# Mixer: the gelus of five returned tiles move a round later, and six weight sums move from the gated unit to the second feed-forward's first pairs

## The chip, the cores and the metric

The kernel runs as one program on one core of a Trainium2 chip. The metric is device time in microseconds. The core has five engines with a queue of instructions each, run in order: TensorE (PE), VectorE (DVE), ScalarE (ACT), GpSimd (POOL) and SyncE (SP). DMAs are issued from the queues of SP, ACT and POOL. The page lists PE's weight loads apart, as PEld.

## The reference

One step of a two-layer streaming encoder in float32 over 1088 positions (1024 of a prompt and 64 of a sample), with D = 1024 channels and a feed-forward of 2816. Layer 0 mixes positions by windowed attention. Layer 1, which the change touches, mixes them by a complex diagonal recurrence (64 groups, 64 states each), then a gelu and a gated linear unit. Each layer ends with a gated feed-forward that has a causal convolution of width 3 on its up-projection.

```python
y = <recurrence over positions> + d_skip * h
z = gelu(y)
ag = z @ w_glu + b_glu
out = ag[..., :D_MODEL] * sigmoid(ag[..., D_MODEL:])
...
up = h @ w_up
c = conv_b + sum(conv_w[j] * shifted(up, j) for j in range(3))
y = (gelu(c[..., :D_FF]) * c[..., D_FF:]) @ w_down
```

Norms (RMS) stand before and after each mixer and each feed-forward.

## The kernel before, in words

**Stages.** In order: attention (layer 0), its feed-forward, the recurrence of layer 1 (in the profile 1190 to 1290 us), the gated unit (1290 to 1493), the second feed-forward's up-projection (from 1493), its down-projection. Every product splits its operands into a high and a low half (hh/hl, zh/zl; weights whl) and runs three matmuls for one (L233 to L235, L1485). Positions go in three blocks of 384, 384 and 320 columns.

**The recurrence.** `ssm` runs batches of two group pairs through a generator, `batch` (L1283 to L1425). The runner `staged` takes every live generator one step per round, the oldest first, so each `yield` puts what follows it behind one more round of all the others. A batch goes through DVE (L1327, L1332, L1333, the scan at L1344, L1347, L1348) with matmuls on PE before (L1293) and after (L1356, L1362, accumulators p3, four buffers). ACT takes p3 out into `ys` (L1370). Every second batch completes a tile of 128 channels, kt = 0 to 7: `ys` is stored to `yd` from ACT's queue (L1377), two yields later it is loaded back in another layout as `yf` by SP (L1383, one yield less for the last tiles), one yield later ACT makes the gelu `z` (L1400 and a small one at L1403), then the high halves `zh` (three copies, L1409); DVE makes the low halves `zl` one yield later (L1424). Tiles 3, 4 and 5 (LATE) leave their `zl` until after the last batch. `ys`, `yf`, `z` of the other tiles, the sums' `sj` and the unit's `sg` all come from one pool, t4, with five buffers, which they take in turn: a new tile waits until the one before it in its buffer has been read by all.

**The gated unit.** 24 tiles (8 columns m by 3 blocks b), 40 to 48 matmuls each (L1485), then a sigmoid `sg` on ACT (L1500) and `y` on DVE (L1501). The last three columns go block by block, so block 0 ends with six tiles to go. At a block's end ACT squares y (sqa, L264), DVE adds the squares (L266, L270) and PE sums them over channels (pr, L276); in PE's order pr stands behind the first matmuls of the next tile. Ahead of each tile and half tile stands one call of `beside` (L1459), which starts one weight sum and finishes one started earlier. A weight sum, `sums(f, e)`, loads two slices of the second feed-forward's up weights on POOL's queue (`sj`, L1446), combines them by four operations of DVE (L1450 to L1453) and stores them to `su` (L1454). The second feed-forward's later pairs use seven products for eight, and read `su` as weights (raw<-su); pairs f = 0 to 4 (PLAIN = 5) are plain. There are 34 sums: f = 5 to 21, two each.

**The second feed-forward.** `gate` (L466) runs once per pair f = 0 to 21. PE makes up-projections into accumulators `mm` (six buffers); DVE takes them out into `u` (L446, L448); the convolution is one operation of ACT and two of DVE (L454 to L456); after the gelu (L469) and the product (L472), POOL stores the result to `gd` (L473, L474). Each convolution is followed by `aside` (L478), which is the place for side work: sums of the down weights, started at given numbers of asides and finished one or two asides later (`sums(j)`, L417, with a table of jobs). In the plain pairs 3 and 4 DVE also forms the normed inputs (L499, L510) and their halves (L492) for the pairs of seven products (L528), which use small pools' tiles t2, t10, t11 among others.

Of the kernel before, what the change touches and what calls it, by code (L numbers as in the profile page):

```python
# [8 lines left out]
F32 = mybir.dt.float32  # L9
# [6 lines left out]
P = 128  # L16
# [6 lines left out]
KF = DFF // P  # L23
# [5 lines left out]
PLAIN = 5  # L29
# [15 lines left out]
class Core:  # L45
# [326 lines left out]
    def ffn(self, i, h, rb, after, side=None, beside=lambda: None, x=None, g=None):  # L372
# [41 lines left out]
        starts.update({2 * (k + KH) + 2: sums_g(k) for k in range(KH)})  # L414
        jobs = {}

        def sums(j):  # L417

            for x in jobs.pop(j, []):
                next(x, None)  # L420
            if j in starts:
                x = starts[j]
                next(x)
                jobs[j + 1 + i] = [x]

        def u_tile(m):
            u = self.t4([P, T + 4], "u")
# [50 lines left out]
        def aside():  # L478

            j = next(turns) + 1  # L480
            if side is not None and j <= SIDE:
                with self.later(LOW):
                    next(side, None)
            sums(j - 1)


        def half(v, j):
# [73 lines left out]
        else:  # L561
            ts_ctx = tc.tile_pool(name="ts", bufs=1)
            ts = ts_ctx.__enter__()
# [673 lines left out]
    def ssm(self, after):  # L1237
# [4 lines left out]
        with tc.tile_pool(name="ss", bufs=1) as sp:  # L1242
# [39 lines left out]
            def batch(qs):  # L1282
# [17 lines left out]
                for c in range(2):  # L1300
                    x = nc.scalar.activation(sc[:, :, c], pm[:, :, OSI:PRM], AF.Copy, scale=(1.0, -1.0)[c])
                    if out[0]:
                        self.order(x, out[0])
                for e, q in enumerate(qs):
                    x = nc.scalar.activation(rd[:, e], mask[:, None, :].to_broadcast([P, 2, 138]), AF.Copy, scale=self.rho[:, q:q + 1])
# [21 lines left out]
                x = nc.vector.tensor_mul(A[:, :, :, 1:], cos[:, :, :, 1:], p1)  # L1327
# [7 lines left out]
                for q in qs:  # L1335
                    if q % 4 == 0 and q < 28:
                        k = q // 4 + 1
                        x = self.ssm_scale(us[k // 2], 8 * (k % 2), 8 * (k % 2) + 8)
# [13 lines left out]
                for i, q in enumerate(qs):  # L1352
                    p3 = [x[:, i] for x in po]
                    for e in range(2):
                        o = OKT + P * e
                        x = nc.tensor.matmul(p3[e], pm[:, i, o:o + P], U(2 * q + e), start=True, stop=False)  # L1356
                    f = self.fill(p1s[-1][:, 0, 2 * NC_:], 1, 512 - 2 * NC_, x) if i == 0 else None
# [17 lines left out]
                if qs[-1] % 4 == 3:  # L1375
                    kt = qs[-1] // 4
                    out.append(nc.scalar.dma_start(yd[kt * P:kt * P + P].rearrange("(g i) t c -> (i t) g c", i=16), ys[0]))  # L1377
                    if kt < 7:
                        yield
                    if kt < 6:  # L1380
                        yield
                    yf = self.t4([P, 8, NC_], "yf")
                    x = nc.sync.dma_start(yf, yd[kt * P:kt * P + P])  # L1383
                    yfs.append(x)
                    self.order(x, got[max(got)])
                    if kt < 7:
                        yield
                    if kt == 6:
                        yield

                        yield
                    if kt == 7:
                        yield
                        yield
                    if kt == LATE[1]:
                        z = self.prep2.tile([P, 2, T], F32, name="z", tag="p2", bufs=1)
                        late[:] = [z[:, x] for x in range(2)]
                    z = late[kt - LATE[1]] if kt in LATE[1:] else self.t4([P, T], "z")
                    yv = yf.rearrange("p t c -> p c t")
                    x = nc.scalar.activation(z[:, 0:SEQ].rearrange("p (c t) -> p c t", t=8), yv[:, 0:128], AF.Gelu_apprx_tanh)  # L1400
                    self.order(x, out[0])
                    self.order(x, out[-1])
                    x = nc.scalar.activation(z[:, SEQ:].rearrange("p (c t) -> p c t", t=8), yv[:, 129:137], AF.Gelu_apprx_tanh)  # L1403
                    self.order(x, out[0])
                    self.order(x, out[-1])
                    for b, (t0, n_) in enumerate(BLK):
                        if kt == 0:
                            zh[b], zl[b] = self.bt(self.blk, b, "zh", F32R), self.bt(self.blk, b, "zl", F32R)
                        nc.scalar.activation(zh[b][:, kt], z[:, t0:t0 + n_], AF.Copy)  # L1409
                    if kt in LATE:  # L1410
                        zs[kt] = z
                        return
                    if kt < 7:
                        yield
                    for b in range(3):
                        x = lower(b, kt, z)
                        if kt < 7:
                            self.order(x, adds[-1])
# [20 lines left out]
        ws = {}  # L1439
        su = self.su = self.dram.tile([KF, 2, P, 2, 512], F32, name="su")  # L1440

        def sums(f, e):

            x = self.t4([P, 2, 2, 256], "sj")
            for j in range(2):
                nc.gpsimd.dma_start(x[:, j], a["w_up"][1, j * KF + f].rearrange("p (c q) -> p c q", c=2)[:, :, 256 * e:256 * e + 256])  # L1446
            yield
            a11, a12, a21, a22 = x[:, 0, 0], x[:, 0, 1], x[:, 1, 0], x[:, 1, 1]
            V = nc.vector
            V.tensor_add(a22, a21, a22)  # L1450
            V.tensor_sub(a21, a11, a21)
            V.tensor_sub(a11, a22, a11)
            V.tensor_sub(a12, a12, a11)  # L1453
            nc.gpsimd.dma_start(su[f, e], x.rearrange("p j c q -> p j (c q)"))  # L1454

        jobs = iter([sums(f, e) for f in range(PLAIN, KF) for e in range(2)])
        loaded = []

        def beside():  # L1459
# [213 lines left out]
```

## Time and profile before

| what | us |
|---|---|
| median of 3 runs (lowest, highest) | 2233.78 (2233.59, 2239.8) |
| the profiled execution | 2242.03 |
| its span on the core | 2240.2 |
| PE, DVE, ACT, POOL busy in it | 2198.9, 1658.0, 1045.6, 410.1 |
| granted clock of PE, mean | 0.993 |

The times in the prediction come from the profiled execution, which took 8.25 us more than the median; 1.8 us of it lie outside the span. In a timeline row stand the start, the busy time, the engine, the line, the operation, what it writes and reads, and how often; in brackets the idle time of the engine just before it and what ended that. In a row of the stretches stand the span, then busy us (and instructions) of PE, PEld, DVE, ACT and POOL, the granted clock, the mean busy share of the 16 DMA engines and GB/s. A group row ends with the summed idle time before its instructions and what ended it. Line numbers are those of the kernel before; in the changed kernel they are 8 to 11 higher.

### The profile page before, as it was taken

Reading aid. Unit: us, or ns where it says so; the run is one execution under the profiler, and the core shown is the slowest. Engines: PE = TensorE matmul, PEld = TensorE weight load, DVE = VectorE, ACT = ScalarE, POOL = GpSimd, SP = SyncE. Lnnn points to the kernel's source line nnn. Section 1 sums busy time; section 2 is a strip of 40 time slices with the busy share of each in tenths; the row PEclk is TensorE's granted clock in tenths of the full one; section 3 lists DMA queues with packets and bytes.
Section 4 is the critical chain, followed back from the end, with each engine's and each line's share of the span. In section 5 each row is a group of like instructions: output and inputs, shape, how many; then the busy total and the mean of one; then the engine's idle time right before and its main releaser. Section 6 shows DMA issues by size and latency. Waiting matters only on the chain.

```text
span 2240.2 us, 36047 instructions
## 1 busy us (share of the span) xinstructions
PE 2198.9 (98%) x13899; PEld 2121.8 (95%) x13899; DVE 1658.0 (74%) x2885; ACT 1045.6 (47%) x1896; POOL 410.1 (18%) x472
## 2 busy tenths in 40 slices
PE   8999999999999999999999899999999999999999
PEld 8987789999999999999986799999999999999998
DVE  8687648989878877767758865588976776676763
ACT  5256747422343342555534741263555455455543
POOL 5322004200132423000200044352010110110000
PEclk9999999999999999999999999999999999999999
DMA  5100015655355565887749888652266686578773
GB/s 197 37 22 29 20 62 158 247 187 202 116 155 173 169 209 186 275 279 230 233 163 344 254 307 291 235 167 75 87 220 233 218 301 222 196 267 312 221 250 102
DMA packets 208123, 428.47 MB, mean 191 GB/s; under 512 B 23312, under 2 KB 114224, under 8 KB 205008
## 3 DMA queue, kind: packets, MB, share of 16 engines
q1 hardware_dynamic: 175648, 326.56, 44.2%
q0 software_dynamic: 23984, 95.12, 11.9%
q10 hardware_dynamic: 8320, 4.49, 0.8%
q8 instruction: 109, 1.79, 0.3%
q14 instruction: 62, 0.51, 0.1%
HBM read 297.75 MB, written 128.37 MB: 190 GB/s over the span
## 4 chain that ended last, share of the span: by engine, by line
PE 29%; DMA 16%; DVE 8%; issue 5%; ACT 3%; POOL 1%; SPq 0%; ACTq 0%; DVEq 0%; POOLq 0%
PE mm L233 9%; PE mm L235 9%; PE mm L234 9%; DMA raw<-in_w_down 4%; DMA sj<-in_w_up 3%; DMA jw<-in_w_down 2%; DMA yf<-yd 1%; DVE whl L222 1%; PE pb L1485 1%; PE pa L1485 1%; ACT whl L221 1%; DMA gr<-gd 1%; DMA pm<-prm 1%; DMA raw<-sd 1%; DVE t L456 1%
## 5 line engine op out<-in xcount | busy, mean ns | idle before, releaser
L233 PE MATMUL mm<-hl,whl 128*128 128x384 f32 (+1 forms) x1960 | 643.0, 329 | 4.0 <-DVE hl L316 2.8
L235 PE MATMUL mm<-hh,whl 128*128 128x384 f32 (+1 forms) x1960 | 640.8, 328 | 2.3 <-DVE whl L222 2.3
L234 PE MATMUL mm<-hh,whl 128*128 128x384 f32 (+1 forms) x1960 | 642.9, 328 | 0.0
L233 PEld LDWEIGHTS mm<-hl,whl 128*128 128x128 f32 x1960 | 368.5, 188 | 6.2 <-DVE hl L316 4.6
L235 PEld LDWEIGHTS mm<-hh,whl 128*128 128x128 f32 x1960 | 368.3, 188 | 3.0 <-DVE whl L222 2.9
L234 PEld LDWEIGHTS mm<-hh,whl 128*128 128x128 f32 x1960 | 368.8, 188 | 0.1
L222 DVE TENSOR_TENSOR whl<-raw,whl 128x1024 fp32r<-128x1024 f32 x202 | 253.7, 1259 | 149.9 <-ACT whl L221 146.5
L221 ACT ACTIVATE whl<-raw 128x1024 fp32r<-128x1024 f32 x202 | 213.1, 1058 | 253.2 <-PE mm L235 131.3
L233 PE MATMUL mm<-gt,whl 128*128 128x384 f32 (+1 forms) x968 | 318.4, 329 | 4.5 <-ACT whl L221 2.9
L235 PE MATMUL mm<-gt,whl 128*128 128x384 f32 (+1 forms) x968 | 316.8, 328 | 0.4 <-DVE whl L222 0.4
L234 PE MATMUL mm<-gt,whl 128*128 128x384 f32 (+1 forms) x968 | 317.0, 328 | 0.0
L233 PEld LDWEIGHTS mm<-gt,whl 128*128 128x128 f32 x968 | 182.7, 189 | 5.7 <-ACT whl L221 3.2
L235 PEld LDWEIGHTS mm<-gt,whl 128*128 128x128 f32 x968 | 182.3, 188 | 1.3 <-DVE whl L222 1.3
L234 PEld LDWEIGHTS mm<-gt,whl 128*128 128x128 f32 x968 | 182.7, 189 | 0.0
L196 DVE TENSOR_TENSOR whl<-raw,whl 128x1024 fp32r<-128x1024 f32 x84 | 96.3, 1153 | 76.5 <-ACT whl L195 75.9
L195 ACT ACTIVATE whl<-raw 128x1024 fp32r<-128x1024 f32 x84 | 82.7, 987 | 105.7 <-DMA raw<-sd 40.7
L455 DVE SCALAR_TENSOR_TENSOR t<-u,ppt,t 128x1090 f32<-128x1090 f32 x88 | 126.7, 1441 | 6.3 <-ACT t L454 4.5
L454 ACT ACTIVATE t<-u,ppt 128x1090 f32<-128x1090 f32 x88 | 114.3, 1298 | 23.9 <-DVE u L551 12.7
L456 DVE SCALAR_TENSOR_TENSOR t<-u,ppt,t 128x1090 f32<-128x1090 f32 x88 | 121.7, 1383 | 0.4
L469 ACT ACTIVATE t<-t 128x1090 f32<-128x1090 f32 x44 | 49.0, 1115 | 114.9 <-DVE t L456 114.8
L446 DVE TENSOR_TENSOR u<-rb,mm 128x384 f32<-128x384 f32 (+1 forms) x164 | 80.2, 501 | 30.4 <-PE mm L235 25.6
L595 DVE TENSOR_TENSOR gt<-gr,gt 128x768 fp32r<-128x768 f32 (+2 forms) x106 | 90.2, 879 | 9.9 <-ACT gt L594 9.4
(392 smaller groups left out, 4072.2 us busy)
## 6 DMA issues: line engine op xcount, KB each, us to landing
raw<-in_w_up SPq DMA_DIRECT2D x88, 512.0 KB, 4.3
raw<-in_w_down SPq DMA_DIRECT2D x74, 512.0 KB, 4.4
raw<-sd SPq DMA_DIRECT2D x40, 512.0 KB, 4.9
sj<-in_w_up POOLq DMA_DIRECT2D x68, 256.0 KB, 6.5
su<-sj POOLq DMA_DIRECT2D x34, 512.0 KB, 5.1
raw<-su SPq DMA_DIRECT2D x34, 512.0 KB, 4.5
pm<-prm SPq DMA_DIRECT2D x32, 522.0 KB, 8.0
gr<-td SPq DMA_DIRECT2D x40, 384.0 KB, 5.7
```

What stands on the lines that cost most here:

```text
L195: nc.scalar.activation(w[:, 0], raw, AF.Copy)
L196: nc.vector.tensor_sub(w[:, 1], raw, w[:, 0].bitcast(F32))
L221: x = [nc.scalar.activation(w[:, 0], raw, AF.Copy)]
L222: low = lambda: nc.vector.tensor_sub(w[:, 1], raw, w[:, 0].bitcast(F32))
L233: nc.tensor.matmul(out, w[:, 0, sl], xl, start=start, stop=False, skip_group_check=more)
L234: nc.tensor.matmul(out, w[:, 0, sl], xh, start=False, stop=False, skip_group_check=more)
L235: self.last_mm = nc.tensor.matmul(out, w[:, 1, sl], xh, start=False, stop=stop, skip_group_check=more)
L446: nc.vector.tensor_mul(u[:, t0 + 2:t0 + 2 + np_], rb[:, t0:t0 + np_], ps[:, :np_])
L454: nc.scalar.activation(t, u[:, 0:T + 2], AF.Identity, bias=cb(m), scale=cw(0, m))
L455: nc.vector.scalar_tensor_tensor(t, u[:, 1:T + 3], cw(1, m), t, op0=ALU.mult, op1=ALU.add)
L456: self.last_conv = nc.vector.scalar_tensor_tensor(t, u[:, 2:T + 4], cw(2, m), t, op0=ALU.mult, op1=ALU.add)
L595: nc.vector.tensor_sub(x[:, 1, u], raw, x[:, 0, u].bitcast(F32))
```

## The change

Two parts, which share no code. In the recurrence, tiles kt = 0 to 4 get two more yields between the load of `yf` and the gelu, which is one round of a tile's two batches. In the sums of the gated unit, the last three pairs (f = 19, 20, 21: six sums) leave the list of jobs. They are kept in `self.rest`, and the second feed-forward starts them at its asides 2 to 5 by two, one, two and one; their tiles come from the buffers t2, t10 and t11, and the four operations on DVE and the store come one aside later. What they compute stays the same.

```diff
--- before.py
+++ after.py
@@ -414,6 +414,14 @@
         starts.update({2 * (k + KH) + 2: sums_g(k) for k in range(KH)})
         jobs = {}
 
+        def rest(j):
+
+            for tag in (("t2", "t10"), ("t11",))[(j - 1) % 2]:
+                x = ts.tile([P, 2, 2, 256], F32, name="sj", tag=tag)
+                job = self.rest.pop(0)(x)
+                next(job)
+                jobs.setdefault(j + 1, []).append(job)
+
         def sums(j):
 
             for x in jobs.pop(j, []):
@@ -421,7 +429,7 @@
             if j in starts:
                 x = starts[j]
                 next(x)
-                jobs[j + 1 + i] = [x]
+                jobs.setdefault(j + 1 + i, []).append(x)
 
         def u_tile(m):
             u = self.t4([P, T + 4], "u")
@@ -482,6 +490,8 @@
                 with self.later(LOW):
                     next(side, None)
             sums(j - 1)
+            if i == 1 and 1 < j < 6:
+                rest(j - 1)
 
 
         def half(v, j):
@@ -1385,7 +1395,7 @@
                     self.order(x, got[max(got)])
                     if kt < 7:
                         yield
-                    if kt == 6:
+                    if kt < 5 or kt == 6:
                         yield
 
                         yield
@@ -1439,9 +1449,9 @@
         ws = {}
         su = self.su = self.dram.tile([KF, 2, P, 2, 512], F32, name="su")
 
-        def sums(f, e):
-
-            x = self.t4([P, 2, 2, 256], "sj")
+        def sums(f, e, x=None):
+
+            x = self.t4([P, 2, 2, 256], "sj") if x is None else x
             for j in range(2):
                 nc.gpsimd.dma_start(x[:, j], a["w_up"][1, j * KF + f].rearrange("p (c q) -> p c q", c=2)[:, :, 256 * e:256 * e + 256])
             yield
@@ -1453,7 +1463,8 @@
             V.tensor_sub(a12, a12, a11)
             nc.gpsimd.dma_start(su[f, e], x.rearrange("p j c q -> p j (c q)"))
 
-        jobs = iter([sums(f, e) for f in range(PLAIN, KF) for e in range(2)])
+        jobs = iter([sums(f, e) for f in range(PLAIN, KF - 3) for e in range(2)])
+        self.rest = [lambda x, f=f, e=e: sums(f, e, x) for f in range(KF - 3, KF) for e in range(2)]
         loaded = []
 
         def beside():
```

On ACT, in the recurrence, tile 0's gelu. The rows start at the store of tile 1 (yd from ys_11780); z is the gelu's result, zh its high halves, ys the evictions, sc, rd and fin small work for the batches. Before:

```order
L1377 DMA yd_11518<-ys_11780 128x8x137
L1400 ACT_TABLE_LOAD
L1400 ACTIVATE z_11873<-yf_11813 128x1024
L1403 ACTIVATE z_11873<-yf_11813 128x64
L1409 ACTIVATE zh_11876<-z_11873 128x384
L1409 ACTIVATE zh_11879<-z_11873 128x384
L1409 ACTIVATE zh_11882<-z_11873 128x320
L1370 ACTIVATE ys_11908<-p3_11885 128x2x137
L1370 ACTIVATE ys_11908<-p3_11886 128x2x137
```

and after the change:

```order
L1387 DMA yd_11518<-ys_11780 128x8x137
L1380 ACTIVATE ys_11896<-p3_11873 128x2x137
L1380 ACTIVATE ys_11896<-p3_11874 128x2x137
...
L1380 ACTIVATE ys_11896<-p3_11931 128x2x137
L1380 ACTIVATE ys_11896<-p3_11932 128x2x137
...
L1387 DMA yd_11518<-ys_11896 128x8x137
L1410 ACT_TABLE_LOAD
L1410 ACTIVATE z_11983<-yf_11813 128x1024
L1413 ACTIVATE z_11983<-yf_11813 128x64
L1419 ACTIVATE zh_11986<-z_11983 128x384
L1419 ACTIVATE zh_11989<-z_11983 128x384
```

The gelu of tile 0 now stands behind two more batches' evictions and behind the store of tile 2 (yd from ys_11896).

On ACT, at the recurrence's end, tiles 4 and 5 (z_12355 before, z_12457 after, two halves of one buffer). Before, tile 4 alone, with the batches' work behind it:

```order
L1400 ACTIVATE z_12355<-yf_12301 128x1024
L1403 ACTIVATE z_12355<-yf_12301 128x64
L1409 ACTIVATE zh_11876<-z_12355 128x384
L1409 ACTIVATE zh_11879<-z_12355 128x384
L1409 ACTIVATE zh_11882<-z_12355 128x320
L1370 ACTIVATE ys_12384<-p3_12361 128x2x137
L1370 ACTIVATE ys_12384<-p3_12362 128x2x137
L1373 COPY fin_11554<-wk_12279 128x8 x2
```

and after:

```order
L1410 ACTIVATE z_12457<-yf_12295 128x1024
L1413 ACTIVATE z_12457<-yf_12295 128x64
L1410 ACTIVATE z_12457<-yf_12402 128x1024
L1413 ACTIVATE z_12457<-yf_12402 128x64
L1419 ACTIVATE zh_11986<-z_12457 128x384
L1419 ACTIVATE zh_11989<-z_12457 128x384
L1419 ACTIVATE zh_11992<-z_12457 128x320
L1419 ACTIVATE zh_11986<-z_12457 128x384
L1419 ACTIVATE zh_11989<-z_12457 128x384
L1419 ACTIVATE zh_11992<-z_12457 128x320
L1380 ACTIVATE ys_12493<-p3_12470 128x2x137
L1380 ACTIVATE ys_12493<-p3_12471 128x2x137
```

The two gelus and their six copies now stand in one stretch, nothing between them, ahead of the next evictions.

On DVE, at the start of the second feed-forward: u are the evictions of the accumulators mm, t the convolution, sj the sums. Before:

```order
L446 TENSOR_TENSOR u_14571<-rb_14172,mm_14784 128x256
L448 TENSOR_TENSOR u_14571<-rb_14172,mm_14784 128x64
L455 SCALAR_TENSOR_TENSOR t_14812<-u_14555,ppt_91,t_14812 128x1090
L456 SCALAR_TENSOR_TENSOR t_14812<-u_14555,ppt_91,t_14812 128x1090
L455 SCALAR_TENSOR_TENSOR t_14818<-u_14563,ppt_91,t_14818 128x1090
L456 SCALAR_TENSOR_TENSOR t_14818<-u_14563,ppt_91,t_14818 128x1090
L472 TENSOR_TENSOR t_14812<-t_14812,t_14818 128x1090
L455 SCALAR_TENSOR_TENSOR t_14829<-u_14571,ppt_91,t_14829 128x1090
L428 MEMSET u_14839 128x2
```

and after, from the same eviction on (a first sum of four operations stands ahead of the evictions):

```order
L454 TENSOR_TENSOR u_14523<-rb_14124,mm_14736 128x256
L456 TENSOR_TENSOR u_14523<-rb_14124,mm_14736 128x64
L1460 TENSOR_TENSOR sj_14783<-sj_14783 128x256
L1460 TENSOR_TENSOR sj_14802<-sj_14802 128x256
L1461 TENSOR_TENSOR sj_14783<-sj_14783 128x256
L463 SCALAR_TENSOR_TENSOR t_14764<-u_14507,ppt_91,t_14764 128x1090
L1461 TENSOR_TENSOR sj_14802<-sj_14802 128x256
L1462 TENSOR_TENSOR sj_14783<-sj_14783 128x256
L464 SCALAR_TENSOR_TENSOR t_14764<-u_14507,ppt_91,t_14764 128x1090
L1462 TENSOR_TENSOR sj_14802<-sj_14802 128x256
L1463 TENSOR_TENSOR sj_14783<-sj_14783 128x256
L1463 TENSOR_TENSOR sj_14802<-sj_14802 128x256
```

Two sums stand among the first convolution's operations; a fourth follows them directly, and the fifth and sixth stand around the next unit's evictions.

## The prediction

> **What bounds the kernel now.** I read the page first, then busy time by stretches for the four stages that the change touches, then in each stretch what waits, then the timeline at those waits. The page's engine line and the by-line half of its chain:
>
> ```profile
> PE 2198.9 (98%) x13899; PEld 2121.8 (95%) x13899; DVE 1658.0 (74%) x2885; ACT 1045.6 (47%) x1896; POOL 410.1 (18%) x472
> ...
> PE mm L233 9%; PE mm L235 9%; PE mm L234 9%; DMA raw<-in_w_down 4%; DMA sj<-in_w_up 3%; DMA jw<-in_w_down 2%; DMA yf<-yd 1%; DVE whl L222 1%; PE pb L1485 1%; PE pa L1485 1%; ACT whl L221 1%; DMA gr<-gd 1%; DMA pm<-prm 1%; DMA raw<-sd 1%; DV
> ```
>
> TensorE (PE) is busy for 98% of the span, so a gain can only come from its few holes. The chain gives the weight sums' loads (sj) 3% and the returned tiles (yf) 1%, together some 90 us. That isn't 90 us to be won; the stretches show why (span, then busy us of PE, PEld, DVE, ACT, POOL, then the granted clock):
>
> ```profile
> 1233.00:1290.00 57.00, 51.17 (x534) 41.12 (x534) 51.51 (x76) 44.99 (x118) 2.80 (x20) 0.97 0.82 252
> 1306.00:1340.00 34.00, 33.25 (x203) 32.99 (x202) 22.26 (x47) 11.14 (x15) 16.36 (x25) 1.00 0.94 338
> ...
> 1380.00:1420.00 40.00, 40.00 (x246) 40.00 (x245) 20.79 (x47) 6.59 (x9) 17.20 (x27) 1.00 0.78 270
> 1420.00:1445.00 25.00, 23.10 (x133) 22.77 (x131) 15.37 (x32) 5.18 (x9) 10.09 (x16) 1.00 0.85 288
> ...
> 1520.00:1600.00 80.00, 80.00 (x492) 79.78 (x492) 66.06 (x100) 32.24 (x45) 8.20 (x10) 1.00 0.23 78
> 1600.00:1680.00 80.00, 79.25 (x485) 78.93 (x484) 67.42 (x85) 41.53 (x64) 8.12 (x14) 1.00 0.52 180
> ```
>
> From 1306 to 1420 the sums wait beside a PE that is full; only 1420 to 1445 has a hole. In the recurrence (1233 to 1290) DVE and PE are both short of full by about 5.5 us. In the second feed-forward (1520 on) PE is full, and DVE has 14 us of 80 free: that is where the six sums go.
>
> **Part A, the gelus.** What waits between 1233 and 1290, the two rows that matter, and the timeline at the first of them (the last row is the store of tile 1, issued at 1228.06, with its microseconds to landing):
>
> ```profile
> ACT z L1400 <- DMA yf<-yd: 12.8, 4, 4.6
> ...
> DVE zl L1424 <- ACT zh L1409: 4.7, 1, 4.7
> ```
> ```profile
> 1228.06 0.37 ACTq L1377 DMA_DIRECT2D yd<-ys  x1
> ...
> 1233.36 2.03 ACT L1400 ACTIVATE z<-yf 128x1024 f32<-128x1024 f32 x1 [3.62 <-DMA yf<-yd]
> ...
> 1230.06 1.31 DVE L1344 TENSOR_TENSOR_SCAN wk<-rd,wk 128x552 f32<-128x552 f32 x1
> 1236.04 1.03 DVE L1424 TENSOR_TENSOR zl<-z,zh 128x384 fp32r<-128x384 f32 x2 [4.67 <-ACT zh L1409]
> ...
> 1242.57 0.73 DVE L1347 TENSOR_TENSOR wk<-wk,pm 128x552 f32<-128x552 f32 x1
> ...
> 1237.11 1.28 PE L1356 MATMUL p<-U,pm 128*128 128x137 f32 x4 [5.34 <-ACT ys L1370]
> ```
> ```profile
> yd<-ys ACTq DMA_DIRECT2D x1, 548.0 KB, 11.3
> ```
>
> ACT waits 12.8 us for returned tiles, but DVE and PE stand still only once, at tile 0: ACT sits in gelu 0's wait, so the evictions (ys) behind it are late for PE (5.34), and DVE sits at tile 0's low halves (zl, 4.67). These are one event seen twice. Elsewhere DVE is full, and the change leaves its operations in the recurrence the same in number. So part A can win at most 4.7.
>
> Does all of it go? In the new order gelu 0 stands behind the store of tile 2, and its buffer (one of five) is now the one that the store of tile 1 reads. That store lands at 1228.06 + 11.3 = 1239.4, so gelu 0 can't start before. From gelu to the first zl took 1236.04 - 1233.36 = 2.7, which puts zl 0 at 1242.1. DVE would come to it, with no gap, at about 1240: the scan ends at 1231.4; a batch is 1242.57 - 1236.04 less 1.4 of zl = 5.1; zl 0 stands two batches on, less the scan and one small addition (1.7). A gap of 2.0 stays; 2.7 is gained. At the end something is given back: gelus 4 and 5 now stand together on ACT ahead of the last evictions but one. The rows of before there:
>
> ```profile
> 1282.68 2.05 ACT L1400 ACTIVATE z<-yf 128x1024 f32<-128x1024 f32 x1
> ...
> 1286.00 0.68 ACT L1370 ACTIVATE ys<-p 128x274 f32<-128x274 f32 x2
> ...
> 1290.59 1.31 PE L1485 MATMUL pb<-zh,whl 128*128 128x384 f32 x6 [0.54 <-ACT ys L1370]
> ```
>
> One tile's gelu and halves take 1286.00 - 1282.68 = 3.3 on ACT, and the unit's first matmul comes 4.6 after that eviction. A second tile ahead of it costs between nothing (it began earlier) and all that was won; I take 0.9, since ACT has by then caught up most of the 3.3. No row shows the pairing. Part A: **-1.8**, bounds -4.7 and 0.
>
> **Part B, six sums less in the gated unit.** A sum is two loads, four DVE additions and a store (group row: busy us, mean ns, then idle before; then us to landing):
>
> ```profile
> L1450 DVE TENSOR_TENSOR sj<-sj 128x256 f32<-128x256 f32 x34 | 14.4, 423 | 50.7 <-DMA sj<-in_w_up 50.3
> ```
> ```profile
> su<-sj POOLq DMA_DIRECT2D x34, 512.0 KB, 5.1
> sj<-in_w_up POOLq DMA_DIRECT2D x62, 256.0 KB, 6.4
> ```
>
> 34 sums fill 1306 to 1443, about 4.1 each, so 28 end about 25 us earlier, three tiles before the first block's end. What that end looks like now:
>
> ```profile
> 1440.09 0.58 ACT L1500 ACTIVATE sg<-pb,ppt 128x384 f32<-128x384 f32 x1 [7.02 <-DMA su<-sj]
> ...
> 1442.86 0.61 DVE L1501 SCALAR_TENSOR_TENSOR y<-pa,ppt,sg 128x384 f32<-128x384 f32 x1
> ...
> 1445.37 0.56 DVE L270 TENSOR_TENSOR sqa<-sqa 128x384 f32<-128x384 f32 x1
> ...
> 1445.98 1.44 PE L276 MATMUL pr<-ones,sqa 128*128 128x1 f32 x6 [2.89 <-DVE sqa L270]
> ```
> ```profile
> 1443.00:1448.00 5.00, 2.11 (x9) 2.02 (x9) 2.49 (x7) 4.35 (x7) 0.53 (x1) 0.72 0.42 171
> 1448.00:1450.00 2.00, 2.00 (x8) 2.00 (x8) 1.38 (x5) 1.65 (x4) 0.00 (x0) 0.50 0.00 0
> 1450.00:1452.00 2.00, 2.00 (x8) 2.00 (x8) 1.50 (x7) 1.37 (x3) 0.00 (x0) 0.50 0.00 0
> 1452.00:1454.00 2.00, 2.00 (x13) 2.00 (x12) 0.85 (x2) 0.95 (x2) 0.00 (x0) 0.99 0.00 0
> ```
>
> The last sigmoid (sg) waits 7.02 for a store of a sum, since both use the same five buffers; the product y comes behind the last additions; and PE, in order, stands 2.89 at the norm's sums (pr). Then it runs at half clock: 8 matmuls in 2 us where 13 follow at 0.99. From 1447.3 to about 1452 that is 4.7 us at half rate, 2.3 lost; the slow pr adds some 0.3. With the sums over early, the chain from sg to pr (0.6 + 0.6 + the squares' 3.1 from 1442.86 to 1445.98, about 4.3 in all) lies beside the next tile's 40 matmuls, which stand ahead of pr in PE's order (the same 13 in 2 us make them 6.2 us). That leaves 1.9 to spare, so the stall goes whole: 2.9 + 2.3 + 0.3 = **-5.5**, bounds -6 and 0.
>
> [...]
>
> **Part B, the same six in the second feed-forward.** 24 additions of 0.42 are 10.1 us more on DVE, by the order ahead of and among the first evictions (u) and convolutions (t), between 1529 and 1560. POOL issues twelve loads and six stores, behind its last work on the operands and ahead of the stores of the gated tiles (gd). PE has no hole there, so the cost is nothing unless DVE falls behind by more than PE's reserve, six accumulators. DVE's gaps, a later eviction, and the matmul that I take to reuse its accumulator; then transfers of that stretch:
>
> ```profile
> 1536.68 0.42 DVE L446 TENSOR_TENSOR u<-rb,mm 128x256 f32<-128x256 f32 x1 [4.72 <-ACT rb L318]
> ...
> 1543.82 1.35 DVE L455 SCALAR_TENSOR_TENSOR t<-u,ppt,t 128x1090 f32<-128x1090 f32 x1 [2.37 <-ACT t L454]
> ...
> 1574.14 0.55 DVE L446 TENSOR_TENSOR u<-rb,mm 128x384 f32<-128x384 f32 x1 [1.61 <-PE mm L235]
> ...
> 1609.16 0.55 DVE L446 TENSOR_TENSOR u<-rb,mm 128x384 f32<-128x384 f32 x1
> ...
> 1615.24 0.34 PE L233 MATMUL mm<-hl,whl 128*128 128x384 f32 x1
> ```
> ```profile
> raw<-in_w_up SPq DMA_DIRECT2D x4, 512.0 KB, 4.0
> gd<-t POOLq DMA_DIRECT2D x3, 512.0 KB, 3.0
> ```
>
> The first sum (1.7) fits the gap of 4.72 if its loads land by 1535. Of the other 8.4, the gaps of 2.37 and 1.61 take 4.0, so DVE is some 4.4 behind at 1575. Behind that it hardly rests, and the tightest place is 1609.7 against 1615.2: a reserve of 5.5. It fits by 1.1. A sum's buffers are three, so the fourth to sixth wait for a store and then a load: 3.0 + 4.0 by these rows, 5.1 + 6.4 by those of the gated unit; the longer pair would put 1 to 3 us of waiting into DVE's queue, behind which evictions stand. Cost: **+0.5**, bounds 0 and +5; below nothing is excluded, as nothing leaves this stage.
>
> [...]
>
> **Sum.** -1.8 - 5.5 + 0.5 = -6.8. The profiled execution took 2242.0 (span 2240.2), so a like one would take 2235.2. The three runs have a median of 2233.8, 8.2 below the profiled one, and the difference is applied to that: **2227.0**.
>
> **Rivals.** (1) Part A wins nothing: the store of tile 1 lands later still, or the paired gelus return all of it. For it: DMA is saturated in the recurrence (0.82 of all engines on average), and 11.3 was the longest landing there. -5.5 + 0.5 = -5.0: 2228.8. (2) Part A wins all 4.7, because that store, issued into less waiting, lands in the usual time and the end keeps its slack: -9.7, 2224.1. (3) The stall at 1445 only shrinks to about 1 us, as the norm's chain itself is late, and the clock still drops: 1.9 won, -3.2 in all, 2230.6. Against it stands the 1.9 of margin. (4) DVE overruns the reserve a little: +3 for +0.5, -4.3, 2229.5. (5) The slow end: each of the three waits for a store and a load (fourth to sixth sum) holds DVE 4 us instead of 1, as with the gated unit's transfers, so DVE is 4.4 + 3 x 4 = 16.4 behind against a reserve of 5.5. PE then stands 11, in two or three gaps that each cost 2.6 of clock as above: +11 + 6 - 7.3 is about +9.7, 2243.5. It decides once the backlog passes 5.5 + 7.3 - 2.6, about 10 us. For it: DVE is in order and an addition that waits holds up the evictions; against it: DMA is only 0.23 busy in 1520 to 1600.
>
> **How the numbers follow.** Forecast 0.40, (1) 0.22, (2) 0.14, (3) 0.07, (4) 0.10, (5) 0.07. About 0.3% or 6.7 us is what a measurement of this kernel can tell from no change, so the line to "faster" is 2227.1, right at the forecast. Faster: all of (2), and rather more than half of the forecast's 0.40, as its own scatter of 1.5 lies on both sides: 0.40. Slower: (5) and a rest of (4): 0.08. The same: 0.52. The range goes from both gains whole at no cost (-10.7, 2223) to part A nothing, half of part B and a cost of 3 to 4 (about +1, 2235), and leaves out (5) and little else.
>
> **What would show it.** Right: no idle PE at the first block's pr and a granted clock of 1.00 there; gelu 0 at about 1239 to 1240 with a wait for a store, DVE's gap before zl 0 about 2; PE full from 1520 to 1680, DVE there at 76 of 80. Wrong: pr still idle; DVE's gap at zl 0 gone or as long as before; PE waiting for u or hl between 1575 and 1640, or a granted clock below 1.00 in that stretch.

## The result, and the profile after

| | runs | median us | lowest, highest |
|---|---|---|---|
| before | 6 | 2236.09 | 2233.59, 2239.8 |
| after | 6 | 2250.86 | 2242.7, 2252.82 |

The ratio of after to before is 1.0061, with a 95% interval of 1.0045 to 1.0077: the changed kernel is slower by 13.6 us (0.0061 x 2236.09), with bounds of 10 and 17. The forecast was 2227.0, faster, and the range ended at 2235. The prediction was wrong in sign, and the result lies outside its range.

The page's engine line of the changed kernel (profiled execution 2251.01, span 2249.2):

```profile
PE 2202.6 (98%) x13899; PEld 2124.1 (94%) x13899; DVE 1652.6 (73%) x2885; ACT 1043.2 (46%) x1896; POOL 409.8 (18%) x472
```

The instructions are the same in number on every engine, and their busy time is the same within 6 us. The span is 9.0 longer than the 2240.2 of before: PE stands idle 5.3 longer (span less busy, 46.6 against 41.3) and takes 3.7 longer for as many matmuls. So the loss is not added work. Where it sits shows in the stretches of after (columns as in the prediction):

```profile
1420.00:1445.00 25.00, 25.00 (x147) 25.00 (x146) 5.34 (x12) 8.35 (x14) 0.00 (x0) 1.00 0.02 8
...
1520.00:1600.00 80.00, 77.71 (x470) 76.82 (x469) 70.63 (x119) 28.43 (x40) 16.72 (x26) 1.00 0.40 140
1600.00:1680.00 80.00, 78.59 (x480) 78.02 (x479) 62.40 (x76) 41.64 (x62) 6.44 (x11) 1.00 0.50 167
1680.00:1760.00 80.00, 77.44 (x464) 76.94 (x463) 53.66 (x66) 39.52 (x70) 9.28 (x16) 0.98 0.67 230
...
2000.00:2220.00 220.00, 212.56 (x1283) 210.72 (x1282) 143.31 (x176) 111.88 (x145) 11.37 (x10) 1.00 0.78 259
```

and the last two of these in the kernel before:

```profile
1680.00:1760.00 80.00, 80.00 (x489) 80.00 (x488) 55.12 (x67) 39.98 (x72) 7.73 (x13) 1.00 0.65 225
2000.00:2220.00 220.00, 219.82 (x1340) 219.51 (x1339) 139.02 (x174) 112.13 (x147) 10.11 (x7) 1.00 0.74 244
```

PE has lost its hole in the gated unit (25.00 of 25, granted clock 1.00), as forecast. It has got holes in the second feed-forward: 2.3 us in the first pairs (1520 to 1600), 2.6 between 1680 and 1760, and 7.4 in the down-projection (2000 to 2220), where before it was full to 0.2. No part of the change touches the last two stretches.

**Part A in the timeline of after.** Tile 0's gelu on ACT, its low halves on DVE, and the first PE rows at the end of the recurrence:

```profile
1236.99 2.07 ACT L1410 ACTIVATE z<-yf 128x1024 f32<-128x1024 f32 x1 [3.39 <-DMA yd<-ys]
...
1239.71 1.03 DVE L1434 TENSOR_TENSOR zl<-z,zh 128x384 fp32r<-128x384 f32 x2 [0.15 <-ACT zh L1419]
...
1285.46 0.79 PE L1366 MATMUL p<-U,pm 128*128 128x137 f32 x4 [3.26 <-ACT ys L1380]
```

The gelu waits for the store of tile 1 (yd<-ys), as the working said it would; that store was issued 2.7 earlier than before, so the gelu comes at 1236.99 and not at 1239.4. DVE's gap of 4.67 is down to 0.15. But 3.26 has appeared on PE at the end, behind an eviction (ys) that stands after the paired gelus. Before, the largest gap there was 0.54.

**The gaps of PE behind the gated unit.** Before had 0.75 at 1629.46, 0.43 and 0.76 at 1789 and 1798, 0.18 at 2193 and 0.46 at 2232. After, in order of time:

```profile
1587.75 0.44 PE L235 MATMUL mm<-hh,whl 128*128 128x384 f32 x1 [1.44 <-DVE whl L222]
...
1685.38 0.44 PE L233 MATMUL mm<-th,whl 128*128 128x384 f32 x1 [2.56 <-DVE u L560]
...
2019.21 0.44 PE L233 MATMUL mm<-gt,whl 128*128 128x384 f32 x1 [1.98 <-DVE gt L605]
...
2117.18 0.83 PE L276 MATMUL pr<-ones,sqa 128*128 128x1 f32 x6 [2.37 <-DVE sqa L270]
```

With those left out here (0.43, 0.43, 0.75, 0.66, 1.05, 0.61, 0.99, 0.45 and 0.47), PE waits 14.2 us behind 1520, where before it waited 2.6. All but 1.6 of it is for DVE.

**Four starts of PE cut the span into stages.** They are the first matmul of the gated unit (pb), of the second feed-forward (hl), of its pairs of seven products (th), and the transposes of the result at the very end (ad from y). All stages below are differences of these starts in one profile each. "Store to pb" runs from the store of tile 0 (yd) on ACT's queue to the first pb, and holds all that part A moves:

| kernel | sums in unit | store to pb | pb to hl | hl to th | th to ad |
|---|---|---|---|---|---|
| before | 34 | 74.52 | 200.54 | 138.33 | 602.56 |
| after | 28 | 75.51 | 195.81 | 141.60 | 614.79 |

From one profile to the other the gated unit gives 4.7 us, the first pairs cost 3.3, and the rest of the second feed-forward costs 12.2. That last one is by far the largest, and the prediction has no term for it.

**What the last column holds.** The kernel's order on each engine is drawn by a list scheduler that follows a timeline of its own when the program is built. With six sums more in the first pairs it draws the second feed-forward anew: of its own instructions, 1877 of 4446 stand at another place on PE, 272 of 652 on DVE, 238 of 546 on ACT and 80 of 213 on SP. Part B by itself brings the new order; part A by itself, and the six sums taken out of the gated unit and put nowhere, leave it as it was. The prediction had read this difference only in the gated unit and the first pairs. Here is DVE around the th product at 1685.38 in after (jw are the sums of the down weights, another side work; u are evictions):

```profile
1675.45 0.69 DVE L390 TENSOR_TENSOR jw<-jw 128x512 f32<-128x512 f32 x1 [6.83 <-DMA jw<-in_w_down]
...
1681.60 0.55 DVE L561 TENSOR_TENSOR u<-u,mm 128x384 f32<-128x384 f32 x1
1682.06 1.22 DVE L222 TENSOR_TENSOR whl<-raw,whl 128x1024 fp32r<-128x1024 f32 x1
1683.51 1.35 DVE L463 SCALAR_TENSOR_TENSOR t<-u,ppt,t 128x1090 f32<-128x1090 f32 x1 [0.23 <-ACT t L462]
1684.78 0.55 DVE L560 TENSOR_TENSOR u<-u,mm 128x384 f32<-128x384 f32 x1
```

and around the same product (there at 1684.91) before:

```profile
1677.43 0.55 DVE L551 TENSOR_TENSOR u<-u,mm 128x384 f32<-128x384 f32 x1 [0.60 <-PE mm L235]
...
1681.39 0.56 DVE L550 TENSOR_TENSOR u<-u,mm 128x384 f32<-128x384 f32 x1 [0.39 <-PE mm L235]
```

Before, both evictions wait for PE, and DVE is done 3 us ahead of the product. After, DVE has stood 6.83 us in front of a load that has not landed, does the same work behind it, and PE waits. The summed waits between 1640 and 1990, first before, then after:

```profile
DVE jw L390 <- DMA jw<-in_w_down: 19.1, 8, 4.7
```
```profile
DVE jw L390 <- DMA jw<-in_w_down: 41.2, 10, 6.8
```

DVE waits twice as long for these loads (41.2 against 19.1). What stands behind them in its queue comes later: the second eviction shown starts at 1684.78, where before it started at 1681.39. The hole behind gt goes back to side work in the same way. DVE waits 3.47 for a load of the sums of the gated tiles (jg), and the gt that PE waits for at 2019.21 comes behind it; before, that sum found its load there at 2005.67. In after:

```profile
2016.54 0.56 DVE L402 TENSOR_TENSOR jg<-jg 128x384 f32<-128x384 f32 x1 [3.47 <-DMA jg<-gd]
...
2018.20 0.95 DVE L605 TENSOR_TENSOR gt<-gr,gt 128x768 fp32r<-128x768 f32 x1
```

### The profile page after: what moved, and what is told of

It reads as the page before. It is cut to its first block, busy times and chain, and to the rows that moved or that the text cites. A ratio compares the mean times of both kernels' runs of the same rounds, so it can differ in the third digit from the quotient of the medians.

```text
span 2249.2 us, 36060 instructions
## 1 busy us (share of the span) xinstructions
PE 2202.6 (98%) x13899; PEld 2124.1 (94%) x13899; DVE 1652.6 (73%) x2885; ACT 1043.2 (46%) x1896; POOL 409.8 (18%) x472
## 4 chain that ended last, share of the span: by engine, by line
PE 36%; DMA 12%; DVE 7%; issue 4%; ACT 3%; POOL 1%; POOLq 0%; SPq 0%; ACTq 0%; DVEq 0%
PE mm L233 9%; PE mm L235 9%; PE mm L234 9%; PE pb L1496 4%; PE pa L1496 4%; DMA raw<-in_w_down 4%; DMA raw<-sd 2%; DMA jw<-in_w_down 1%; DMA yd<-ys 1%; DVE whl L196 1%; DVE whl L222 1%; ACT whl L195 1%; DMA pm<-prm 1%; ACT whl L221 1%; DMA yf<-yd 1%
## 5 line engine op out<-in xcount | busy, mean ns | idle before, releaser
L604 ACT ACTIVATE gt<-gr 128x768 fp32r<-128x768 f32 (+2 forms) x106 | 78.3, 772 | 39.7 <-DMA gr<-gd 27.2
```

## The experiments

All ratios are against the kernel before on the same chip; 0.001 is 2.24 us. In the kernels that hold the second feed-forward to a given order, a wrapper issues the instructions, so most of their lines read L57. The order is held like this, for PE, DVE, ACT and SP, by dependencies that give an order and no wait of their own. The kernel before, held to its own order, was not run; the run with the transfers alone is held in this way and measured -1.6, so the holding itself has no cost that shows.

```diff
+def pin(c, seen):
+    for e, text in ORDER.items():
...
+        for j, k in zip(ks, ks[1:]):
+            c.tc.add_manual_dep(v[k], v[j].name, dep, reason="order")
```

### Part A alone

```diff
-                    if kt == 6:
+                    if kt < 5 or kt == 6:
```

> Part A alone: the gelus a round later, all 34 sums in the gated unit. The instruction order behind the recurrence is that of before on every engine. If the prediction's part A holds, -1.8 us. By the profile of after (the recurrence was entered 2.7 us ahead of before and left 1.7 ahead), +1.0. If part A were what made the kernel slower, about +13.

Measured: 2233.84, ratio 0.9991 (0.9975 to 1.0007): -2.0 us, not to be told from nothing. Two rows of its profile, the stretch with the first block's end and the gap at the end of the recurrence:

```profile
1440.00:1450.00 10.00, 10.00 (x62) 9.96 (x61) 4.62 (x17) 5.16 (x9) 0.00 (x0) 1.00 0.00 1
```
```profile
1283.40 0.89 PE L1356 MATMUL p<-U,pm 128*128 128x137 f32 x4 [1.81 <-ACT ys L1370]
```

Two things follow. The end of the recurrence gives back part of what the start gained (1.61 and 3.46 in the other two profiles with part A). And this kernel still makes 34 sums in the gated unit, yet PE has no hole at the first block's end and the clock is 1.00: the stall of 2.89 on which the largest term rested isn't there in this execution.

### The last six sums left out

This kernel leaves six sums uncomputed; the pairs that need them read those of an earlier pair. The order of the second feed-forward is that of before.

```diff
-        jobs = iter([sums(f, e) for f in range(PLAIN, KF) for e in range(2)])
+        jobs = iter([sums(f, e) for f in range(PLAIN, KF - 3) for e in range(2)])
```

> 28 sums in the gated unit, and the last six not computed at all (the pairs 19 to 21 read the sums of pair 18 in their place), no part A; the order of all other instructions is that of before. Every theory expects the gated unit's gain alone: -4.7 (as the profile of after has it) to -5.5 (as predicted). Nearer 0 would say that the stall of before's profile is not in its usual runs.

Measured: 2234.24, ratio 0.9988 (0.9974 to 1.0003): -2.7 us (-5.8 to +0.7). So taking six sums out of the gated unit, at no cost anywhere, is worth about half of the forecast 5.5 by the medians; the interval holds both nothing and 5.5.

### Part B with the second feed-forward in its old order

Part B in full, and the order of all other instructions of the second feed-forward held to that of before.

> Part B with the second feed-forward's own instructions held, by order-only dependences, to the order they have before the change on PE, DVE, ACT and SP; the six sums stand in the same place as in the changed kernel. Theory order (the changed kernel is slower because the scheduler redrew the whole rest of the second feed-forward): -2 to -5. Theory load (24 additions on DVE and 18 transfers on POOL's queue in the first pairs cost it directly): +8 to +12. PE's idle from 1660 on should be below 2 us by order, 10 by load.

Measured: 2243.29, ratio 1.0029 (1.0016 to 1.0043): +6.5 us. The profiled execution was the fastest of its runs (2234.57). The same kernel again, in two runs on another chip, with a profile of an ordinary execution:

> The six sums with the old order once more, for a second profile: the first one was the fastest of its runs (2234.6, median 2243.3). [...]

Measured: 2247.49, ratio 1.0050 (1.0032 to 1.0067). The additions have a price of their own, in the old order too. It shows mainly at one place. DVE and PE there, in the second profile:

```profile
1610.00:1620.00 10.00, 10.00 (x66) 10.00 (x65) 10.00 (x12) 4.95 (x5) 1.07 (x2) 1.00 0.31 108
1620.00:1630.00 10.00, 10.00 (x67) 10.00 (x66) 9.99 (x10) 4.02 (x7) 0.00 (x0) 1.00 0.37 110
1630.00:1640.00 10.00, 5.79 (x24) 5.47 (x23) 7.91 (x12) 5.68 (x10) 1.80 (x3) 0.83 0.41 119
```
```profile
1634.69 1.80 PE L57 MATMUL mm<-th,whl 128*128 128x384 f32 x7 [4.21 <-ACT u L57]
...
1622.16 1.23 DVE L57 TENSOR_TENSOR whl<-raw,whl 128x1024 fp32r<-128x1024 f32 x1
...
1621.82 1.98 SPq L57 DMA_DIRECT2D raw<-su  x2
...
1629.79 1.06 ACT L57 ACTIVATE whl<-raw 128x1024 fp32r<-128x1024 f32 x1 [3.22 <-DMA raw<-su]
1630.76 2.41 ACT L57 ACTIVATE hh<-y 128x1280 fp32r<-128x1280 f32 x2
...
1634.16 0.48 ACT L57 ACTIVATE u<-mm 128x384 f32<-128x384 f32 x1
```

and the same links before:

```profile
1629.46 0.45 PE L233 MATMUL mm<-th,whl 128*128 128x384 f32 x1 [0.75 <-ACT u L540]
...
1617.15 1.21 DVE L222 TENSOR_TENSOR whl<-raw,whl 128x1024 fp32r<-128x1024 f32 x1
...
1616.80 1.97 SPq L199 DMA_DIRECT2D raw<-su  x2
...
1622.97 1.06 ACT L221 ACTIVATE whl<-raw 128x1024 fp32r<-128x1024 f32 x1 [0.84 <-DMA raw<-su]
```

Both profiles start the second feed-forward at the same time (1491.08 and 1491.13), and DVE is by now 5.0 us later than before (1622.16 against 1617.15). The two loads of the next weights (raw<-su) take their buffers as DVE reads them out, and start 5.0 later (1621.82 against 1616.80); the second of them, behind the read shown, also lands after 6.3 us and not after 4.5. ACT, in order, stands 3.22 in front of them instead of 0.84; the last halves (hh), a gelu and the eviction (u) stand behind that, and the first th product waits for the eviction: 4.21 instead of 0.75. This place had no reserve before the change. The first profile has the same stall with 3.45.

### The new order without the change

The kernel before, with neither part, and the second feed-forward held to the order that it has in the changed kernel. Nothing is added, moved between stages or left out.

> The kernel before, neither part of the change in it, with the second feed-forward's instructions held to the order that they have in the changed kernel. Theory order: +8 to +12, with PE stalls at the seven-product pairs and in the down-projection as in the changed kernel's profile. Theory load: within 2 us of before.

Measured: 2252.69, ratio 1.0057 (1.0035 to 1.0079): +12.7 us (+7.8 to +17.7), about as much as the whole change. The profiled execution was the slowest of its runs (2260.21). Its stretches, the DVE wait from above, and three of its gaps:

```profile
1680.00:1760.00 80.00, 75.71 (x456) 74.66 (x456) 54.06 (x67) 36.36 (x62) 9.34 (x16) 1.00 0.64 215
2000.00:2220.00 220.00, 213.71 (x1263) 212.03 (x1262) 144.88 (x180) 112.10 (x146) 11.87 (x11) 0.98 0.76 255
```
```profile
DVE jw L57 <- DMA jw<-in_w_down: 46.0, 10, 6.0
```
```profile
1687.00 2.38 PE L57 MATMUL mm<-th,whl 128*128 128x384 f32 x12 [1.74 <-DVE u L57]
...
2123.04 1.10 PE L57 MATMUL pr<-ones,sqa 128*128 128x1 f32 x6 [1.91 <-DVE sqa L57]
...
2164.30 4.00 PE L57 MATMUL mm<-gt,whl 128*128 128x320 f32 x15 [1.88 <-DVE y L57]
```

The hole at the th product and all but one of those of the down-projection stand at the same products with the same releasers as in the changed kernel, though in other sizes, and the wait for the loads is as long. Between 1700 and 1810 this profile has five more holes (0.34 to 1.69), for u from DVE as well. The order alone makes such holes.

### The additions on GpSimd

As part B in the old order, with the six sums' four operations moved from DVE to POOL.

```diff
+            V = nc.vector if x is None else nc.gpsimd
```

> As the run with the six sums in the old order, but their 24 additions are GpSimd's instead of DVE's; same loads and stores at the same place, no part A. If DVE's queue is what the six sums cost in the first pairs, the time falls to that of the run without them, about -3 us against before. If the transfers (or POOL's queue, in which the stores of the gated tiles now stand behind additions too) are the cost, it stays at +6 or more.

Measured: 2249.88, ratio 1.0042 (1.0024 to 1.0060): +9.4 us, no better than on DVE. Groups of POOL in 1520 to 1640, then of DVE in 1545 to 1610, then that DVE group before:

```profile
L1491 POOL TENSOR_TENSOR sj<-sj 128x256 f32<-128x256 f32 x6 | 7.6, 1263 | 0.0
...
L1489 POOL TENSOR_TENSOR sj<-sj 128x256 f32<-128x256 f32 x6 | 5.2, 866 | 4.6 <-DMA sj<-in_w_up 4.6
```
```profile
L57 DVE SCALAR_TENSOR_TENSOR y<-y,ppt,rb 128x384 f32<-128x384 f32 x16 | 12.1, 824 | 0.0
```
```profile
L499 DVE SCALAR_TENSOR_TENSOR y<-y,ppt,rb 128x384 f32<-128x384 f32 x16 | 8.6, 609 | 0.0
```

An addition takes 0.87 to 1.26 us there, where DVE takes 0.42 (423 ns in the gated unit before), and DVE's own operation of the same form in the stretch takes 824 ns instead of 609. Two other groups of DVE in the same stretch keep their time (whl 1218 ns against 1219, u of 384 columns 548 in both). Why the one is slower these rows don't show. The stage from hl to th takes 149.39 us, against 139.12 with the transfers alone (table by stage below).

### The transfers without the additions

As part B in the old order, without the 24 additions: the loads are stored back as they came, so six sums are not formed.

```diff
+            if not adds:
+                nc.gpsimd.dma_start(su[f, e], x.rearrange("p j c q -> p j (c q)"))
+                return
```

> The same with the 24 additions left out: the loads go into the tiles and are stored to su as they came, so the last three pairs use sums that were not formed. Old order, no part A. DVE theory: -3 us, as without the six. Transfers theory: +6, as with them.

Measured: 2238.02, ratio 0.9993 (0.9980 to 1.0005): -1.6 us. The first th product waits 0.75, as before. The twelve loads and six stores cost nothing that shows.

### One sum at a time, later

The six sums go one by one into pairs 5 to 10, every second aside; the order of all else is that of before. Without part A, then with it:

```diff
+            if i == 1 and j in range(12, 24, 2):
+                rest(j - 1)
```

> The six sums go one at a time into the pairs 5 to 10 (one buffer, t2, every second aside), where DVE has 10 us of 40 free, instead of the plain pairs; old order, no part A. If it is the crowding of DVE ahead of the seven-product pairs that costs, -3 to 0 us. If the sums cost 9 us wherever they stand in this stage, +6.

> The same with part A (the gelus a round later): the whole change, with its sums at another place and the order held. If the parts add up, -5 to -2 us against before, since part A alone came to about -2.

Measured: 2242.04, ratio 1.0010 (0.9997 to 1.0022), +2.2 us; with part A 2241.42, ratio 1.0012 (1.0002 to 1.0023), +2.7 us. The stall at the first th is back to 0.75, and others come at later ones, 1.24, 0.67 and 1.60 in the first of the two. Spread out, the additions cost less by the medians (+2.2 against +6.5, with intervals that overlap), but neither version is faster than before.

### Part B alone, in the order that the scheduler gives it

> Part B alone, the order left to the scheduler (it comes out as in the changed kernel from the second feed-forward on). If part A adds its own -2 and nothing else, the whole change less part A: +12 to +18 us against before. If it is the two parts together that make the changed kernel slow, less than +8.

Measured: 2252.95, ratio 1.0077 (1.0064 to 1.0091): +17.2 us. So part A isn't what makes the changed kernel slow, and the whole change (+13.6) is if anything a little better than its part B.

### The additions once their loads have landed

As part B in the old order, with each sum's operations placed one or two operations later in DVE's queue, so that they find their loads there.

```diff
+        if e == "vector":
+            for n, (j, k) in enumerate(((17, 18), (21, 22), (21, 22), (24, 51), (32, 34), (32, 34))):
```

> The six sums at the same asides with the old order, but each sum's four additions stand on DVE one or two operations later, where their loads have landed, so that DVE does not wait for them (6.2 us of such waits in the profile of the first such run). If the waits are what the sums cost, -2 to +1 against before; if the additions' own 10 us are, +5 to +7 as before.

Measured: 2242.11, ratio 1.0029 (1.0018 to 1.0041): +6.5 us, the same as with the waits. The stretch with the first th:

```profile
1620.00:1630.00 10.00, 6.49 (x30) 6.17 (x29) 9.80 (x13) 5.55 (x9) 0.71 (x1) 0.85 0.36 113
```

PE waits 3.51 there for the same eviction. What costs is the 10 us of DVE work, not the waits for its loads.

### The whole change in the old order

Parts A and B, the second feed-forward held to its old order.

> The whole change, both parts and the sums where the change puts them, with the order of the second feed-forward held to that of before. What it lies below the changed kernel is what the redrawn order costs. Theory order and load together: +4 to +7 against before. Theory load alone: +12 to +15. Theory order alone: -5 to -2.

Measured: 2240.57, ratio 1.0016 (1.0005 to 1.0028): +3.6 us. The down-projection and the wait for the loads in it:

```profile
2000.00:2220.00 220.00, 218.40 (x1335) 218.09 (x1334) 138.76 (x174) 110.00 (x145) 9.40 (x7) 1.00 0.72 237
```
```profile
DVE jw L57 <- DMA jw<-in_w_down: 18.5, 8, 3.6
```

With the old order the wait is back to that of before (19.1), and PE's holes between 2000 and 2220 fall from 7.4 to 1.6. The same two edits cost 13.6 with the redrawn order and 3.6 without it.

### All profiles by stage

| kernel | store to pb | pb to hl | hl to th | th to ad |
|---|---|---|---|---|
| A alone (34 sums) | 75.65 | 194.49 | 139.13 | 600.54 |
| six left out | 75.97 | 194.89 | 139.15 | 601.78 |
| B, old order | 75.12 | 194.39 | 142.59 | 600.56 |
| the same again | 76.52 | 194.62 | 143.61 | 603.42 |
| before, new order (34 sums) | 76.76 | 195.74 | 140.07 | 621.02 |
| additions on POOL | 76.30 | 194.76 | 149.39 | 600.39 |
| transfers only | 74.88 | 194.98 | 139.12 | 600.42 |
| spread late | 75.85 | 194.69 | 139.12 | 605.10 |
| spread late, and A | 77.48 | 195.74 | 139.13 | 607.05 |
| B alone, new order | 75.18 | 195.52 | 141.28 | 619.29 |
| after their loads | 75.67 | 195.27 | 143.44 | 604.74 |
| A and B, old order | 73.70 | 195.24 | 142.60 | 604.35 |

The stages tell more than the totals, since the start of pb itself lies between 1286.93 and 1297.97 in profiles that differ little ahead of it; that is the scatter of one execution, and it is as large as the effects looked for. The last column has two groups: 600 to 607 in the old order, 615 to 621 in the new one, whether or not the sums are there. How far apart they are is not settled by these profiles: the 621.02 and 619.29 are from the slowest runs of their kernels (2260.21 and 2263.97, medians 2252.69 and 2252.95), and only the 614.79 of the changed kernel is from an ordinary one. In the third column, in the old order, 138.3 to 139.2 without additions in the first pairs becomes 142.6 to 143.6 with them on DVE, and 149.4 with them on POOL.

## Why the prediction was wrong

**The step that failed most is one that isn't written out.** The sum had three terms (-1.8, -5.5, +0.5), all of them at places that the edits touch, and took everything behind the first pairs to stay as it was. The redrawn order of the second feed-forward is worth about +10 us: after less the same edits in the old order, 13.6 - 3.6 = 10.0; part B in its two orders, 17.2 - 6.5 = 10.7; the order by itself, 12.7. The two later runs of part B in the old order, at 1.0050 (+11.2) on the chip of the 17.2, would make the second of these 6.0, so the estimates lie between 6 and 13. None of the rivals held it. The difference of the two orders could be read beforehand, and on PE it reaches to place 3827 of the 4446; it was compared only as far as the first pairs. What could not be read from it is the sign. That the price of the order is DVE's longer wait for the loads of the down weights, and that this causes the late u, is read from the timeline at one product and from the sums of waits (19.1 and 18.5 in the old order, 41.2 and 46.0 in the new); a kernel with only those additions moved back was not tried. The hole behind gt goes back to a load of side work too, and those behind sqa were traced to DVE alone, not further.

**"It fits by 1.1": the reserve was read at the wrong place.** The backlog of 4.4 us on DVE was about right (5.0 at 1622). The reserve of 5.5 was that of an accumulator at 1615. The tightest place is the first th product at 1629, which waited 0.75 already: it hangs on ACT, ACT on a load of weights, and the load on the buffer that DVE frees. There the reserve is nothing. The predicted cost was +0.5 with bounds of 0 and +5. The profiles give +3.5 to +4.5 in the stage that holds it (142.6 to 143.6 against 139.1). The medians give more: part B in the old order less the six left out +9.2, and less the transfers alone +8.1, each with some 4 either way. The stage is thus at the low end of what the medians allow, and what the rest of their difference is stays open.

**The gated unit, -5.5: the place and the mechanism were right, the size was that of one execution.** Between the two profiles the stage gives 4.7 (200.54 to 195.81). But the kernel before was profiled in an execution of 2242.03, with a median of 2236.09, and two kernels that still make all 34 sums take 194.49 and 195.74, with gaps of none and 1.04 at the first block's end. A stall that comes in some executions can't be counted whole against the median: leaving the six sums out measures -2.7 (-5.8 to +0.7), within the bounds of -6 and 0 and half the value taken; the interval still holds 5.5.

**Part A, -1.8: rival (1) is nearer.** The wait for the store was forecast and is there; the DVE gap went almost wholly instead of to 2.0 (0.15, and 0.86 with part A alone), and the end of the recurrence gave back 3.26 and 1.81 instead of 0.9. By the stage from the first store to pb the four profiles with part A have a mean of 75.6 and the ten without it 75.7 (with before and after among them). The medians give -2.0 (-5.6 to +1.6) alone. All agree with nothing won, and none excludes 2.

**Rival (5)** had the sign and a stage, at a chance of 0.07, but its mechanism is refuted: additions that find their loads landed cost as much (+6.5 and +6.5), and the loads without additions cost nothing. The waits were there (DVE stood 6.2 us in front of these loads in the first profile of part B in the old order), but the kernel without them is no faster. Of the signs that were named for "wrong", two came true in the changed kernel: DVE's gap at zl 0 is gone, and PE waits for u between 1575 and 1640, though only 0.43 at 1585.74 (the 1.44 at 1587.75 is for weights, whl).

No version tried is faster than before by more than its interval. Of those that compute everything, part A alone, with all 34 sums where they were, is the nearest, at 0.9991.

## What to carry to other kernels

Where a scheduler draws the order from a timeline of its own, an edit in one stage can redraw every stage behind it: compare the orders to the program's end, and give the stretches that changed a term or a rival of either sign, even if no instruction in them was edited. To learn what the edit itself is worth, hold the rest to its old order, and run the old program in the new order as well: the two together separate work from order. Look for a reserve along the chain that hangs on the delayed engine by way of other queues and of buffers, not only at the accumulators, and don't count a stall of one profiled execution against a median from which that execution is 6 us away.

## What the runs showed of the hardware

The granted clock fell behind some of PE's gaps here and not behind others that were longer: it was 0.57 behind gaps of 1.88 and 1.91 us, 0.66 behind 2.56 and 0.62 behind 3.51, but 1.00 behind 2.37 and 3.45. These are the 4 us (5 in the first) behind four gaps: 2.56 in after, 2.37 in after, then 1.91 and 1.88 in the kernel before with the new order (first two rows of after, then two of the other):

```profile
1685.00:1690.00 5.00, 4.62 (x18) 4.62 (x19) 2.75 (x5) 2.31 (x3) 0.71 (x1) 0.66 0.68 202
...
2117.00:2121.00 4.00, 3.82 (x24) 3.82 (x25) 2.55 (x4) 1.51 (x2) 0.00 (x0) 1.00 0.89 298
```
```profile
2123.00:2127.00 4.00, 3.96 (x16) 3.96 (x17) 2.44 (x3) 1.36 (x2) 0.00 (x0) 0.57 0.85 274
...
2164.00:2168.00 4.00, 3.70 (x15) 3.70 (x16) 1.91 (x5) 3.23 (x5) 0.00 (x0) 0.57 0.49 145
```

The 2.37 and the 1.91 stand at the same product (pr): 24 matmuls followed in 4 us behind the longer gap, 16 behind the shorter. The stall at the first th product shows it with two gaps of nearly one length, 3.45 in the first profile of part B in the old order and 3.51 in the one with the additions after their loads:

```profile
1624.00:1628.00 4.00, 3.85 (x22) 3.85 (x23) 4.00 (x9) 1.14 (x5) 0.71 (x1) 1.00 0.08 32
```
```profile
1626.00:1630.00 4.00, 3.85 (x14) 3.85 (x15) 4.00 (x9) 0.80 (x4) 0.71 (x1) 0.62 0.24 45
```

The first keeps its clock, with 22 matmuls in 4 us, and the second has 14. So length alone doesn't decide it in these runs; what else does, they don't show.
